# Gelu and sigmoid of a mixing phase by hyperbolic tangents, tile by tile, with the sums of the gated output asked for earlier

## The chip, the core and the metric

The program runs on one core of a Trainium2 chip. [...] An engine waits for another on semaphores. The metric is the device time of one execution in microseconds. Before the change three runs took 2308.72 to 2311.48 us, median 2311.45.

## The reference

One layer of a streaming encoder on 2048 tokens of 1024 features, float32. An input projection feeds two halves of 512 features: a state-space layer and chunked attention. The part that the change touches is what lies between them and the output projection:

```python
y = jax.nn.gelu(y.reshape(bsz, seq, D_SSM))                      # tanh form
y = y * jax.nn.sigmoid(y @ w_glu.astype(f32) + b_glu.astype(f32))
...
mixed = jnp.concatenate([rmsnorm(y_ssm, norm_ssm_out_g[l]),
                         rmsnorm(y_att, norm_att_out_g[l])], axis=-1)
x = x + mixed @ w_out[l]
```

After it come a SwiGLU layer, a residual and a last norm, which the change leaves as they are.

## The kernel before

Features lie on the 128 partitions, tokens along the free dimension. The mixing (mix_phase, from line 973) works on four blocks of 512 tokens, each with four tiles of 128 features (f or q from 0 to 3). Products that need float32 are made of a high and a low part (hi/lo, gh/gl, woh/wol): split makes the high part on ACT and the low part, raw minus high, on DVE or POOL; mm3 issues three matrix products (high by high, low weight or input by high).

For a block, load reads y, the state-space output, into yr, applies Gelu into ys and splits it into gh and gl. yr has its tokens in the order (j, c) and ys in the order (c, j), so Gelu's instruction reads yr in steps. load_a reads ya, the attention output, and squares makes its sum of squares over the four tiles: Squares on ACT, additions on DVE and, for tile 2, on POOL. glu multiplies by w_glu (4 tiles, each 4 quarters of 3 products, into ps), applies the sigmoid gate to ys, and calls squares on it. rstd1 sums the squares over the partitions (products with ones, into PSUM) and runs newton on DVE: 14 small steps, from nv to no, that give 1/rms. spread brings no to all partitions by PE, and rstd2 multiplies ys or ya by it and by the gain. mixed splits the outcome into m, and w_out multiplies m by the output weights, adds xt and stores x.

Tiles of one name share buffers in turn: sg has SGB = 2. sg holds the raw gate weights, the terms of squares and, in blocks 2 and 3, the gate.

Blocks 0 and 1 begin while attention still runs. There glu is called with late: the four tiles of ps get their bias on DVE and are put into yr; after the fourth, one instruction of ACT takes the sigmoid of all four, and DVE multiplies. load makes one instruction of Gelu over four tiles. In blocks 2 and 3 both go tile by tile. Gelu, Sigmoid and attention's Exp belong to different function tables of ACT; where the function changes, an ACT_TABLE_LOAD stands in its order.

What sets the order: PE's instructions keep the order in which the code is written. attention's loop runs in steps, and mix_phase is a generator whose yields are spread over the last steps, so that glu's quarters lie among scores (sc), transposes of the exponentials (pt), products with v (pj). In a step DVE makes scores plus bias and their minimum (s, mn), ACT the Exp, PE pt, ACT and DVE the high and low parts pth and ptl; for a pair of heads yt (ACT) and ya (DVE) follow. The other engines' instructions are placed by a scheduler when the program is built, and then run in that order. The sub-steps of block 1's glu are counted: at number R1 the sums of block 0's gated output are asked for (line 1171). Behind block 1's glu, w_out of block 0 starts with the attention half of m; the state-space half needs the spread.

## Time and profile before

| what | value |
|---|---|
| median of three runs | 2311.45 us |
| the profiled execution | 2304.9 us |
| its span, first to last instruction | 2303.1 us |
| mean clock of PE | 0.975 |
| ACT_TABLE_LOAD on ACT | 9, of 1.283 us each |
| the mixing, about | 686 to 950 us |

In the profile, a row of a timeline has start and length in us, engine, line, operation, tile written and tiles read, partitions by elements and a count; in brackets the idle time of the engine just ahead of it and what released it. A row of a group has the total, the mean in ns of one instruction, and the idle time ahead of them. A row of a table by stretches has each engine's busy time and, as PEclk, the share of full clock that PE was granted.

### The profile page before, as it was taken

Reading aid. Unit: us, or ns where it says so; the run is one execution under the profiler, and the core shown is the slowest. Engines: PE = TensorE matmul, PEld = TensorE weight load, DVE = VectorE, ACT = ScalarE, POOL = GpSimd, SP = SyncE. Lnnn points to the kernel's source line nnn. Section 1 sums busy time; section 2 is a strip of 40 time slices with the busy share of each in tenths; the row PEclk is TensorE's granted clock in tenths of the full one; section 3 lists DMA queues with packets and bytes.
Section 4 is the critical chain, followed back from the end, with each engine's and each line's share of the span. In section 5 each row is a group of like instructions: output and inputs, shape, how many; then the busy total and the mean of one; then the engine's idle time right before and its main releaser. Section 6 shows DMA issues by size and latency. Waiting matters only on the chain.

```text
span 2303.1 us, 30454 instructions
## 1 busy us (share of the span) xinstructions
PE 2183.8 (95%) x10568; PEld 1834.1 (80%) x10568; DVE 1487.8 (65%) x2286; ACT 1001.3 (43%) x1675; POOL 1061.0 (46%) x1245
## 2 busy tenths in 40 slices
PE   8978799999997899989999999999999999999997
PEld 6667688898986788778888887888888878888886
DVE  7845555656555756676775669766645376578676
ACT  6335555555557542343333335333333343344332
POOL 3416655455660433265555554555555314445442
PEclk9989999999998999999999999999999999999998
DMA  8788766766653534754554556555433287465552
GB/s 295 260 286 265 235 210 204 207 190 193 192 137 114 178 118 163 249 165 143 167 193 157 205 190 254 195 193 167 158 96 110 76 326 265 165 228 183 201 182 74
DMA packets 216370, 437.00 MB, mean 190 GB/s; under 512 B 27352, under 2 KB 58120, under 8 KB 209112
## 3 DMA queue, kind: packets, MB, share of 16 engines
q1 hardware_dynamic: 211352, 420.89, 55.0%
q0 software_dynamic: 4864, 14.17, 1.9%
q8 instruction: 83, 1.36, 0.2%
q14 instruction: 71, 0.58, 0.1%
HBM read 294.98 MB, written 132.15 MB: 185 GB/s over the span
## 4 chain that ended last, share of the span: by engine, by line
PE 59%; DVE 3%; DMA 1%; ACT 1%; issue 1%; POOL 1%; SPq 0%; DVEq 0%; ACTq 0%; POOLq 0%
PE X L74 20%; PE ps L74 18%; PE Y L74 10%; PE big L74 6%; PE W L74 5%; DVE acc L1575 1%; DMA lo<-hc 0%; DMA x<-xt 0%; DVE xt L1117 0%; DVE lo L166 0%; DVE hd L166 0%; POOL c L166 0%; ACT hi L165 0%; POOL sa L1125 0%; DMA gl<-x 0%
## 5 line engine op out<-in xcount | busy, mean ns | idle before, releaser
L74 PE MATMUL X<-hi,c 128*128 128x512 f32 x1408 | 452.2, 392 | 7.6 <-ACT u L1391 3.5
L74 PE MATMUL ps<-hd,hd 128*128 128x512 f32 (+1 forms) x1968 | 431.7, 381 | 3.9 <-DVE hd L166 3.7
L74 PEld LDWEIGHTS ps<-hd,hd 128*128 128x128 f32 x1968 | 358.8, 190 | 75.5 <-DVE hd L166 5.1
L166 POOL TENSOR_TENSOR c<-S,c 128x512 fp32r<-128x512 f32 x176 | 253.1, 1440 | 260.7 <-ACT c L165 258.8
L74 PEld LDWEIGHTS X<-hi,c 128*128 128x128 f32 x1408 | 265.8, 189 | 65.2 <-ACT u L1391 5.1
L74 PE MATMUL X<-lo,c 128*128 128x512 f32 x704 | 275.3, 391 | 0.0
L166 POOL TENSOR_TENSOR hd<-hd 128x1536 fp32r<-128x1536 f32 (+1 forms) x46 | 159.1, 3463 | 232.0 <-ACT hd L165 218.8
L166 POOL TENSOR_TENSOR c<-raw,c 128x512 fp32r<-128x512 f32 x132 | 189.0, 1432 | 137.5 <-ACT c L165 109.1
L165 ACT CAST hd<-hd 128x1536 fp32r<-128x1536 f32 (+1 forms) x106 | 147.4, 1393 | 219.4 <-DMA hd<-hq 134.5
L74 PE MATMUL Y<-hi,c 128*128 128x512 f32 x704 | 225.5, 391 | 4.8 <-DVE u L1395 4.8
L1521 DVE TENSOR_TENSOR acc<-acc,ps 128x512 f32<-128x512 f32 x196 | 129.2, 681 | 79.5 <-PE ps L74 79.1
L74 PE MATMUL big<-m,woh 128*128 128x512 f32 x512 | 165.4, 404 | 0.6 <-DVE m L166 0.4
L165 ACT CAST c<-S 128x512 fp32r<-128x512 f32 x176 | 109.5, 622 | 116.5 <-PE Y L74 59.1
L74 PE MATMUL pf<-hi,w 128*128 128x512 f32 x416 | 150.9, 415 | 9.4 <-ACT hi L729 5.8
L74 PEld LDWEIGHTS Y<-hi,c 128*128 128x128 f32 x704 | 132.6, 188 | 33.9 <-DVE u L1395 6.3
L74 PEld LDWEIGHTS X<-lo,c 128*128 128x128 f32 x704 | 133.0, 189 | 27.7
L1391 ACT COPY u<-X 128x512 f32<-128x512 f32 x132 | 77.1, 585 | 177.5 <-PE X L74 177.5
L846 DVE CUSTOM_DVE_ANT_0 s<-sc,nb 128x640 f32<-128x640 f32 (+4 forms) x128 | 94.4, 737 | 89.4 <-PE sc L74 85.9
L605 POOL TENSOR_TENSOR st<-X,a 128x128 f32<-128x128 f32 (+2 forms) x136 | 47.4, 349 | 220.0 <-ACT X L591 157.4
L165 ACT CAST c<-raw 128x512 fp32r<-128x512 f32 x132 | 82.1, 622 | 143.1 <-PE Y L74 80.3
L166 DVE TENSOR_TENSOR hd<-hd 128x1536 fp32r<-128x1536 f32 (+1 forms) x60 | 119.3, 1990 | 31.2 <-ACT hd L165 30.5
L74 PE MATMUL Y<-lo,c 128*128 128x512 f32 x352 | 137.2, 390 | 0.0
(462 smaller groups left out, 4644.2 us busy)
## 6 DMA issues: line engine op xcount, KB each, us to landing
w<-wss SPq DMA_DIRECT2D x36, 1024.0 KB, 5.5
hq<-g SPq DMA_DIRECT2D x140, 256.0 KB, 2.1
hd<-hq SPq DMA_DIRECT2D x42, 768.0 KB, 4.5
hd<-wc SPq DMA_DIRECT2D x42, 768.0 KB, 6.0
raw<-in_w_gate SPq DMA_DIRECT2D x44, 512.0 KB, 3.7
raw<-in_w_up SPq DMA_DIRECT2D x44, 512.0 KB, 4.1
wc<-px SPq DMA_DIRECT2D x66, 256.0 KB, 3.2
wss<-w SPq DMA_DIRECT2D x12, 1024.0 KB, 5.6
```

Of the source, the lines that this page charges most:

```text
L74: return self.tc.keep_in_program_order(self.tc.nc.tensor.matmul(*a, **b))
L165: (hi_eng or nc.scalar).copy(hi, raw)
L166: (lo_eng or nc.gpsimd).tensor_tensor(lo, raw, f32(hi), op=ALU.subtract)
L605: eng.tensor_tensor(t[:, :, :, :n], src, ar, op=ALU.mult)
L846: nc.vector.tensor_tensor_reduce(s[:, :nk].rearrange("p (a b) -> p a b", a=nch), ps[:, :nch, :half], hd.nb[:, nk - 1 :: -1].rearrange("p ( ...
L1391: nc.scalar.copy(u[:], ps[:])
L1521: V.tensor_tensor(a, a, ps[:], op=ALU.add)
L1575: nc.vector.scalar_tensor_tensor(v, v, k.go[:, i : i + 1], self.rs[:, : self.n], op0=ALU.mult, op1=ALU.mult)
```

## The change

Gelu's tanh form is written out: a Square of y on ACT, a product on DVE that also adds 1/0.044715, a Tanh on ACT, a product on DVE (tanh plus one, times y), which gives twice the Gelu. gh is then a scaled copy, and gl is made with a scale of 0.5 in its subtraction. The sigmoid is half of one plus tanh of half its argument: a Tanh on ACT that reads ps, with half the bias, and a product on DVE. So ys holds four times the gated output; a scale in squares and a quarter of the gain gs make up for it. Both go tile by tile in all blocks, the intermediate t and the gate in sg; yr no longer holds the gate. The instructions read yr in blocks of 64, and the second product writes ys in steps of eight elements. R1 goes from 13 to 9. The built program has two ACT_TABLE_LOADs, at the start and at Silu.

```diff
@@ -33,7 +33,8 @@
 LAG = 2
 WB = 3
 OPEN, GSTART = 119, 122
-R1 = 13
+R1 = 9
+CUBE = 0.044715
 SGB = 2
 ON_POOL = 2, 5, 7
 RA1, RA2 = 2, 12
@@ -982,6 +983,8 @@
         nc.sync.dma_start(gs[:], io["g_ssm"])
         nc.sync.dma_start(ga[:], io["g_att"])
         nc.sync.dma_start(bg[:], io["b_glu"])
+        nc.vector.tensor_scalar(gs[:], gs[:], 0.25, None, op0=ALU.mult)
+        nc.vector.tensor_scalar(bg[:], bg[:], 0.5, None, op0=ALU.mult)
         BIG = ("big", [P, 1024])
         W, Wg = {}, {}
 
@@ -1003,14 +1006,14 @@
                 raw = raws[n] if n < len(raws) else load_wo(n, wr, "xt")
                 split(k, W[q][0][:], W[q][1][:], raw[:], nc.vector if n % 2 else nc.gpsimd)
 
-        def squares(src):
+        def squares(src, scale=1.0):
             sq = k.t(mz, "sq", [P, SB], bufs=2)
             for f in range(4):
                 if f == 0:
-                    nc.scalar.activation(sq[:], src[f], AF.Square)
+                    nc.scalar.activation(sq[:], src[f], AF.Square, scale=scale)
                 else:
                     t = k.t(mz, "sg", [P, SB], bufs=SGB)
-                    nc.scalar.activation(t[:], src[f], AF.Square)
+                    nc.scalar.activation(t[:], src[f], AF.Square, scale=scale)
                     (nc.gpsimd if f == 2 else nc.vector).tensor_tensor(sq[:], sq[:], t[:], op=ALU.add)
             return sq
 
@@ -1019,7 +1022,7 @@
 
         yrs = [None]
 
-        def load(sb, one=False):
+        def load(sb):
             b = B()
             b.o = {}
             yt = k.t(my, "ys", [P, 4, SB], bufs=2)
@@ -1028,13 +1031,16 @@
                 yrs[0] = k.t(my, "yr", [P, 4, L, 128])
                 for f in range(4):
                     nc.sync.dma_start(yrs[0][:, f], S["y"][f * P : (f + 1) * P, :, sb * 64 : sb * 64 + 128])
-            yv = b.yr = yrs[0][:, :, :, (sb % 2) * 64 : (sb % 2 + 1) * 64]
-            fs = [slice(0, 4)] if one else [slice(f, f + 1) for f in range(4)]
-            for s in fs:
-                nc.scalar.activation(yt[:, s].rearrange("p f (c j) -> p f c j", j=L), yv[:, s].rearrange("p f j c -> p f c j"), AF.Gelu_apprx_tanh)
+            yv = yrs[0][:, :, :, (sb % 2) * 64 : (sb % 2 + 1) * 64]
             for f in range(4):
+                t = k.t(mz, "sg", [P, L, SB // L], bufs=SGB)
+                nc.scalar.activation(t[:], yv[:, f], AF.Square)
+                nc.vector.scalar_tensor_tensor(t[:], t[:], 1 / CUBE, yv[:, f], op0=ALU.add, op1=ALU.mult)
+                nc.scalar.activation(t[:], t[:], AF.Tanh, scale=CUBE * math.sqrt(2 / math.pi))
+                nc.vector.scalar_tensor_tensor(b.ys[f].rearrange("p (c j) -> p j c", j=L), t[:], 1.0, yv[:, f], op0=ALU.add, op1=ALU.mult)
                 gh, gl = k.t(my, f"gh{f}", [P, SB], F32R), k.t(my, f"gl{f}", [P, SB], F32R)
-                split(k, gh[:], gl[:], b.ys[f], nc.vector)
+                nc.scalar.activation(gh[:], b.ys[f], AF.Copy, scale=0.5)
+                nc.vector.scalar_tensor_tensor(gl[:], b.ys[f], 0.5, f32(gh[:]), op0=ALU.mult, op1=ALU.subtract)
                 b.g.append((gh, gl))
             return b
 
@@ -1044,11 +1050,7 @@
                 nc.sync.dma_start(b.ya[f], S["ya"][sb, f * P : (f + 1) * P])
             b.sqa = squares(b.ya)
 
-        def glu(b, bank, late=False):
-
-
-            def by8(a):
-                return a.rearrange("p (a b) -> p a b", a=L)
+        def glu(b, bank):
 
             for f in range(4):
                 ps = bank()
@@ -1057,18 +1059,11 @@
                     mm3(te, ps[:, :512], Wg[q][0][:, cs], Wg[q][1][:, cs], b.g[q][0][:], b.g[q][1][:], q == 0, q == 3)
                     if q < 3:
                         yield
-                if late:
-                    nc.vector.tensor_scalar(b.yr[:, f], by8(ps[:, :512]), bg[:, f : f + 1], None, op0=ALU.add)
-                    if f == 3:
-                        nc.scalar.activation(b.yr, b.yr, AF.Sigmoid)
-                        for i in range(4):
-                            nc.vector.tensor_tensor(by8(b.ys[i]), by8(b.ys[i]), b.yr[:, i], op=ALU.mult)
-                else:
-                    sg = k.t(mz, "sg", [P, SB], bufs=SGB)
-                    nc.scalar.activation(sg[:], ps[:, :512], AF.Sigmoid, bias=bg[:, f : f + 1])
-                    nc.vector.tensor_tensor(b.ys[f], b.ys[f], sg[:], op=ALU.mult)
+                sg = k.t(mz, "sg", [P, SB], bufs=SGB)
+                nc.scalar.activation(sg[:], ps[:, :512], AF.Tanh, bias=bg[:, f : f + 1], scale=0.5)
+                nc.vector.scalar_tensor_tensor(b.ys[f], sg[:], 1.0, b.ys[f], op0=ALU.add, op1=ALU.mult)
                 yield
-            b.sqs = squares(b.ys)
+            b.sqs = squares(b.ys, 0.25)
 
         def rstd1(b, c, ps):
 
@@ -1145,12 +1140,12 @@
         yield
         mw = rx.enter_context(tc.tile_pool(name="mw", reuse_waits="tile", bufs=2, side="right"))
         wr = rx.enter_context(tc.tile_pool(name="wr", reuse_waits="tile", bufs=2, side="right"))
-        b = load(0, True)
+        b = load(0)
         load_a(b, 0)
         raws = [load_wo(n, wr, "xt") for n in range(2)]
         for _ in range(PY):
             yield
-        for n, _ in enumerate(glu(b, bank, True)):
+        for n, _ in enumerate(glu(b, bank)):
             if n == RA1:
                 rstd1(b, 0, bank())
             if n == RA2:
@@ -1158,7 +1153,7 @@
                 spread(k, te, pb, b.o[0], 0)
                 rstd2(b, 0, pb[:])
             yield
-        nxt = load(1, True)
+        nxt = load(1)
         for _ in range(PZ):
             yield
 
@@ -1167,7 +1162,7 @@
             psum = k.psum
             return bank() if psum is None else big()
 
-        for n, _ in enumerate(glu(nxt, bk, True)):
+        for n, _ in enumerate(glu(nxt, bk)):
             if n == R1:
                 rstd1(b, 1, bk())
             yield
```

What the scheduler made of it, at three places. First DVE among the last steps of attention, behind the splits of the gate weights (wgl); ISA is the instruction that makes s and its minimum mn; the numbers in the names are those of buffers and differ between the two programs. Before:

```order
L166 TENSOR_TENSOR wgl_1899_8231<-sg_8232,wgh_1898_8230 128x512
L166 TENSOR_TENSOR wgl_1902_8237<-sg_8238,wgh_1901_8236 128x512
L889 TENSOR_TENSOR ya_8144<-pj_8314,yt_8331 64x512
L846 ISA s_8401,mn_8402<-sc_8396,nb_8133 128x640
L846 ISA mn_8402 128x1
L865 TENSOR_TENSOR ptl_8335<-pt_8336,pth_8334 128x5x128
L898 TENSOR_TENSOR ya_8144<-ya_8144,pj_8405 128x512
L846 ISA s_8425,mn_8426<-sc_8420,nb_8299 128x640
L846 ISA mn_8426 128x1
L865 TENSOR_TENSOR ptl_8335<-pt_8412,pth_8334 128x5x128
L865 TENSOR_TENSOR ptl_8335<-pt_8429,pth_8334 128x5x128
```

and now:

```order
L167 TENSOR_TENSOR wgl_1902_8239<-sg_8240,wgh_1901_8238 128x512
L1038 SCALAR_TENSOR_TENSOR sg_8358<-sg_8358,yr_8353 128x512
L1038 SCALAR_TENSOR_TENSOR sg_8367<-sg_8367,yr_8353 128x512
L890 TENSOR_TENSOR ya_8144<-pj_8316,yt_8333 64x512
L1040 SCALAR_TENSOR_TENSOR ys_8352<-sg_8358,yr_8353 128x8x64
L866 TENSOR_TENSOR ptl_8337<-pt_8338,pth_8336 128x5x128
L1040 SCALAR_TENSOR_TENSOR ys_8352<-sg_8367,yr_8353 128x8x64
L1043 SCALAR_TENSOR_TENSOR gl_1931_8364<-ys_8352,gh_1930_8363 128x512
L1038 SCALAR_TENSOR_TENSOR sg_8376<-sg_8376,yr_8353 128x512
L1043 SCALAR_TENSOR_TENSOR gl_1934_8373<-ys_8352,gh_1933_8372 128x512
L847 ISA s_8422,mn_8423<-sc_8417,nb_8133 128x640
L847 ISA mn_8423 128x1
```

Seven instructions of block 0's Gelu (lines 1038, 1040, 1043) have come ahead of the next minimum, in front of which only ya stood.

Second, ACT: Gelu and the high parts of block 1. Before, directly behind block 0's, ahead of the first Exp that follows (the sq and sg rows are Squares of the attention output):

```order
L165 CAST gh_1935_8369<-ys_8350 128x512
L1013 ACTIVATE sg_8383<-ya_1938_8374 128x512
L1013 ACTIVATE sg_8386<-ya_1939_8375 128x512
L1034 ACTIVATE ys_8631<-yr_8351 128x2048
L1013 ACTIVATE sg_8389<-ya_1940_8376 128x512
L849 ACT_TABLE_LOAD
L849 ACTIVATE s_8449,sm_8249<-s_8449,mn_8450 128x640
```

and now, behind the last gate tile of block 0 (sg from pf, line 1063) and the Squares of its gated output (line 1016):

```order
L1063 ACTIVATE sg_8641<-pf_8611,bg_8214 128x512
L1016 ACTIVATE sg_8646<-ys_8352 128x512
L1016 ACTIVATE sg_8649<-ys_8352 128x512
L1016 ACTIVATE sg_8652<-ys_8352 128x512
L1037 ACTIVATE sg_8656<-yr_8353 128x512
L1037 ACTIVATE sg_8665<-yr_8353 128x512
L889 COPY yt_8713<-pj_8696 64x512
L1039 ACTIVATE sg_8656<-sg_8656 128x512
L1039 ACTIVATE sg_8665<-sg_8665 128x512
L1042 ACTIVATE gh_1999_8661<-ys_8655 128x512
L1037 ACTIVATE sg_8674<-yr_8353 128x512
L1042 ACTIVATE gh_2002_8670<-ys_8655 128x512
```

Block 1's Gelu has moved from ahead of block 0's gate to behind it.

Third, DVE: the newton steps for block 0's gated output, among splits of the output weights (wol) and block 1's gate. Before:

```order
L1061 TENSOR_SCALAR yr_8351<-big_8709,bg_8214 128x8x64
L166 TENSOR_TENSOR wol_2031_8823<-m_2017_8792,woh_2030_8822 128x1024
L1061 TENSOR_SCALAR yr_8351<-big_8723,bg_8214 128x8x64
L115 TENSOR_SCALAR nv_8749<-big_8744 128x4
L166 TENSOR_TENSOR wol_2035_8831<-m_2019_8796,woh_2034_8830 128x1024
L116 CAST nf_8750<-nv_8749 128x4
L1061 TENSOR_SCALAR yr_8351<-big_8737,bg_8214 128x8x64
L117 TENSOR_SCALAR nf_8750<-nf_8750 128x4
L119 TENSOR_SCALAR nv_8749<-nv_8749 128x4
L118 CAST ny_8751<-nf_8750 128x4
```

and now:

```order
L1064 SCALAR_TENSOR_TENSOR ys_8655<-sg_8751,ys_8655 128x512
L167 TENSOR_TENSOR wol_2043_8861<-xt_8415,woh_2042_8860 128x1024
L1064 SCALAR_TENSOR_TENSOR ys_8655<-sg_8767,ys_8655 128x512
L116 TENSOR_SCALAR nv_8782<-big_8777 128x4
L117 CAST nf_8783<-nv_8782 128x4
L118 TENSOR_SCALAR nf_8783<-nf_8783 128x4
L120 TENSOR_SCALAR nv_8782<-nv_8782 128x4
L119 CAST ny_8784<-nf_8783 128x4
L122 TENSOR_TENSOR nf_8783<-ny_8784 128x4
L123 TENSOR_TENSOR nf_8783<-nf_8783,nv_8782 128x4
L124 SCALAR_TENSOR_TENSOR no_8785<-nf_8783,ny_8784 128x4
```

The additions of the bias (line 1061) are gone, products by the gate (line 1064) have come, and nv stands ahead of the second wol of these rows instead of the third. On PE the sums (four products of ones with sq) now stand behind the second quarter of block 1's tile 2, not the second of tile 3; PE's order is otherwise as it was. On SP the loads of y for block 2 stand ahead of those of xt.

## Prediction

> **What bounds the kernel now.** I read the page's busy times and its chain that ended last, then a table by stretches around the mixing, then the timelines of each engine there.
>
> ```profile
> PE 2183.8 (95%) x10568; PEld 1834.1 (80%) x10568; DVE 1487.8 (65%) x2286; ACT 1001.3 (43%) x1675; POOL 1061.0 (46%) x1245
> PE 59%; DVE 3%; DMA 1%; ACT 1%; issue 1%; POOL 1%; SPq 0%; DVEq 0%; ACTq 0%; POOLq 0%
> core 0: us, PE busy (x) PEld busy (x) DVE busy (x) ACT busy (x) POOL busy (x), PEclk, DMA share, GB/s
> 698.00:721.30 23.30, 10.89 (x44) 8.46 (x42) 10.41 (x18) 18.83 (x22) 1.28 (x1) 0.63 0.54 183
> ...
> 743.30:762.00 18.70, 18.01 (x83) 14.13 (x81) 17.92 (x18) 12.52 (x17) 14.45 (x7) 1.00 0.61 220
> 762.00:767.40 5.40, 0.29 (x3) 0.05 (x1) 5.09 (x16) 2.18 (x2) 2.50 (x1) 0.95 0.27 85
> 767.40:790.00 22.60, 21.34 (x95) 17.32 (x96) 17.24 (x23) 17.58 (x27) 7.79 (x5) 0.94 0.50 158
> 790.00:900.00 110.00, 109.75 (x504) 91.19 (x503) 62.96 (x141) 41.24 (x59) 36.77 (x26) 0.98 0.41 134
> ```
>
> TensorE is the bound and the chain is mostly its own work. The change can gain only where PE stands still in the mixing: 12.4 us of 698 to 721 and 5.1 us of 762 to 767. From 790 to 900 PE is never idle. Elsewhere the change can only cost. PE's waits in full:
>
> ```profile
> 701.72 1.00 PE L77 MATMUL pt<-ident,s 128*128 128x128 f32 x5 [2.42 <-DVE ptl L865]
> ...
> 705.54 1.30 PE L77 MATMUL pt<-ident,s 128*128 128x128 f32 x5 [1.75 <-DVE ptl L865]
> 713.61 0.79 PE L74 MATMUL pf<-gh,wgh 128*128 128x512 f32 x1 [6.76 <-ACT gh L165]
> ...
> 715.35 0.63 PE L74 MATMUL pf<-gh,wgh 128*128 128x512 f32 x1
> 715.78 0.63 PE L74 MATMUL pf<-gl,wgh 128*128 128x512 f32 x1
> ...
> 721.26 1.05 PE L74 MATMUL pf<-ones,sq 128*128 128x1 f32 x8 [1.47 <-DVE sq L1014]
> ...
> 739.29 0.40 PE L74 MATMUL pf<-gh,wgl 128*128 128x512 f32 x1
> ...
> 743.35 0.48 PE L74 MATMUL big<-gh,wgh 128*128 128x512 f32 x1
> ...
> 755.86 0.40 PE L74 MATMUL big<-gh,wgl 128*128 128x512 f32 x1
> ...
> 767.38 1.09 PE L77 MATMUL big<-ident,no 128*128 128x128 f32 x4 [5.11 <-DVE no L123]
> ...
> 788.39 1.05 PE L74 MATMUL big<-ones,sq 128*128 128x1 f32 x8 [1.16 <-DVE nv L115]
> ```
>
> A matmul of 512 columns follows the last after 0.43 us at the low clock (715.35, 715.78); 48 of them and the sums take 12.9 us at full clock (743.35 to 756.2), about 0.23 us each.
>
> ```profile
> L849 ACT ACTIVATE s<-s,mn 128x640 f32<-128x640 f32 x96 | 79.9, 833 | 51.8 <-DVE mn L846 51.5
> L864 ACT CAST pth<-pt 128x640 fp32r<-128x640 f32 x96 | 66.6, 693 | 59.9 <-PE pt L77 58.5
> ...
> 707.59 1.28 ACT L1034 ACT_TABLE_LOAD   x1
> 708.88 3.64 ACT L1034 ACTIVATE ys<-yr 128x2048 f32<-128x2048 f32 x1
> ...
> 712.95 2.16 ACT L165 CAST gh<-ys 128x512 fp32r<-128x512 f32 x4
> 716.07 3.83 ACT L1034 ACTIVATE ys<-yr 128x2048 f32<-128x2048 f32 x1
> ...
> 776.40 1.28 ACT L1034 ACT_TABLE_LOAD   x1 [1.11 <-issue]
> ...
> 826.30 1.28 ACT L1068 ACT_TABLE_LOAD   x1
> ...
> 700.00 0.82 DVE L846 CUSTOM_DVE_ANT_0 s<-sc,nb 128x640 f32<-128x640 f32 x1
> ```
>
> The 6.8 us wait is a table load (1.28), one Gelu over four tiles (3.64), and gh. Yet block 1's Gelu (716.07) also runs here, 27 us before PE needs it at 743.35: that cover the change gives up. Four of the seven table loads that go, those of blocks 2 and 3 (776.40 to 826.30), fall where PE hardly waits: they are worth nothing.
>
> **Prices.** The new instructions by their nearest rows:
>
> ```profile
> L1013 ACT ACTIVATE sg<-ys 128x512 f32<-128x512 f32 x12 | 7.4, 632 | 5.3 <-DVE ys L1069 4.7 <-DVE sq L1014 0.6
> L1082 DVE SCALAR_TENSOR_TENSOR ys<-ys,gs,big 128x512 f32<-128x512 f32 x16 | 10.8, 737 | 0.0
> 746.85 1.29 POOL L1014 TENSOR_TENSOR sq<-sq,sg 128x512 f32<-128x512 f32 x1 [28.65 <-DVE sq L1014]
> L1117 DVE TENSOR_TENSOR xt<-xt,big 128x1024 f32<-128x1024 f32 x16 | 19.4, 1214 | 38.6 <-PE big L74 29.3 <-DMA xt<-in_xt 9.2
> L88 ACT COPY rsn<-pb 128x512 f32<-128x512 f32 x4 | 4.9, 1222 | 0.1
> L88 ACT COPY pb<-pp 128x512 f32<-128x512 f32 x4 | 2.3, 587 | 26.6 <-PE pp L77 26.6
> ```
>
> A Square, tanh or scaled copy on ACT is 0.63 us (0.52 apart in a row: 2.16 for four gh). A plain product on DVE is 0.74 (0.66 apart: 10.8 us for 16), an addition on POOL 1.29. The two scalings of gs and bg are four columns wide (nv below, as wide, takes 0.14): nothing. Per block DVE gets eight more instructions (products), of which four write ys with a step of eight elements. The trace has no such write on DVE; the nearest is ACT's copy to rsn, which steps by eight (1.22 us against 0.59 for a plain one). So such a product lies between 0.74 (as if plain) and 1.48 (twice); I take 1.22.
>
> [...]
>
> **Term A, block 0, up to the sums of the attention output (PE row 721.26): +2.3.** (sc are scores, pt their transposes, ptl the low part, exp the softmax's exponential.) The added DVE rows stand between wgl and the softmax's next minimum: five plain (0.66) and two stepped (1.22), 5.7 us. The minimum moves from 700.0 to 706.1, and the third pt behind it (ptl, exp, one more stepped product) from 705.5 to 709.4. PE then finds gh and gl of tiles 0 and 1 ready, so the 6.8 us wait goes: six matmuls at 0.43, scores and pt (about 1.05 each at this clock, as at 701.72), until 715.3. But ACT's order puts the Squares of the attention output behind the third exp; pth (0.69) and that exp (0.83) follow on this pt, until 716.9. From there: Square 0.6, product 0.7, tanh 0.65, stepped product 1.25, gh 0.6, Square 0.6, POOL 1.3, DVE 0.75, handoffs: 723.6 against 721.3. The first wait is replaced by one of about 7 us on the sums. From there to the last gate matmul (739.7) PE works without a break; DVE trades four bias additions for four products. So that end, T0, is 742.0.
>
> **Term B, block 1: +9.9.** Its Gelu uses the two sg buffers, behind the gate and the squares of block 0, so it can't start before T0. The chain: tanh 742.7, product 743.5, Square of the third tile 744.2, POOL's addition 745.6 (frees sg), Square 746.3, product 747.05, tanh behind yt 748.1, ya 748.35, stepped product 749.6, gh 750.2. PE's cover, the last attention products, ran from 739.7 to 743.35: until 745.65 now. Then DVE has, in order, a stepped product (to 750.75), ya (751.3), two gl (752.55), two products (753.8), two stepped (756.3), m (756.95), two gl (758.2). PE ends the first gate tile at 759.1, in pieces, at the low clock. Six more matmuls at 0.43 and 30 at 0.23 end at 768.4; before it was 756.2. That is 12.2 late, of which 2.3 is term A.
>
> **Term C, the sums of the gated output: −6.1.**
>
> ```profile
> 759.54 0.14 DVE L115 TENSOR_SCALAR nv<-big 128x4 f32<-128x4 f32 x1
> 759.61 2.70 DVE L166 TENSOR_TENSOR wol<-m,woh 128x1024 fp32r<-128x1024 f32 x1
> 762.23 2.30 DVE L116 CAST nf<-nv 128x4 f32<-128x4 int32 x1
> 764.44 0.74 DVE L1061 TENSOR_SCALAR yr<-big,bg 128x512 f32<-128x512 f32 x1
> ...
> 767.07 0.16 DVE L123 SCALAR_TENSOR_TENSOR no<-nf,ny 128x4 f32<-128x4 f32 x1
> ```
>
> Newton's 14 steps were asked for late and stood among two weight splits and a bias addition, so PE waited 5.1 us at 767.38. Now the sums come after gate tile 2's second quarter (about 765), the steps end near 770, and PE wants them at 768.4 plus the first half of the first output product (24 matmuls, 5.6): 774.0. The wait goes, with 1.0 of the 1.4 us that clock 0.94 over 22.6 us cost behind it. Next late is then m of the gated output, which PE wants 5.5 us later, as before; it costs what it did.
>
> **Term E, the pair of sums at 788.39: +1.3.** PE writes the second sums only when DVE's nv has read the first. From the spread at 774.0 PE needs 0.7, 24 and 48 matmuls (16.6 with the stalls on m that the row pattern has today, 1.2), and 0.9 for the first sums: 793.4. DVE makes the four gains until 780.3 (they stand behind POOL's addition of block 1's squares), two m and an addition until 782.9, then block 2's products: four plain 2.65, four stepped 4.9, two gl 1.3; then two additions to x (1.2 each) and two gl (1.3) stand before nv: 795.6. A wait of about 2.5 in place of 1.16. Blocks 2 and 3 have 20 to 30 us of cover for gh (PE never idle from 790 to 900): nothing. Without that cover block 3 would pay block 1's price. SP's queue: yr is free once ys is made, so block 2's loads of y go ahead of those of xt; both are wanted 25 us later: nothing.
>
> **Sum.** +2.3 +9.9 −6.1 +1.3 = +7.4 us. The profiled execution took 2304.9 (span 2303.1 and 1.8 around it): 2312.3. The median of the runs, 2311.45, lies 6.55 above that execution, so I forecast 2318.9. With stepped products at 1.48 the eleven in the way (3, 4, 4) add 2.9: 2321.8.
>
> **Rivals.**
> - Stepped writes cost 0.74. A is −0.5 (sums at 720.8), B +8.1 (gate ends 763.8 from T0 739.2), C −6.1, E 0: +1.5, 2313.0. For it: no row on DVE speaks against it. Against: the copy to rsn, and Gelu itself, which reads in steps (3.64 for 2048 elements).
> - Faster: the first wait really goes. DVE was free for 12.9 of the 23.3 us from 698 to 721. If the products fall into those holes, PE gets from 706.8 to the sums by 714.7, A is −6.6, and with PE busy there the clock of 0.63 recovers for 1.5 more: −8.1 +8.1 −6.1 +0 = −6.1, 2305.4. It decides whether the attention output's sums are ready before 715. Against it: those Squares stand behind the third exp.
> - Newton is still last, between two products that wait for tanh: C is 0, +13.5, 2325. Against it: PE has 8 us of work behind tile 2.
>
> That the table loads stay is excluded: the built order has two where there were nine.
>
> **How the numbers follow.** Forecast 0.48 (2315 to 2323), plain writes 0.25 (2309 to 2316), faster 0.20 (2302 to 2309), Newton 0.07. From 2307 to 2323 only 0.15 of the third case and 0.05 at the top are left out. This kernel's measurement tells 0.2% (4.6 us) from no change: below 2306.8 lies 0.15 (third case); above 2316.1 lie 0.41 of the forecast and 0.07 of the last, 0.48; within, 0.37.
>
> **What would show it.** A: PE waits some 7 us for sq ahead of the first sums, none for gh before. B: waits for gh and gl at block 1's first gate tile, with a lower clock up to 760. C: no wait before the first spread of block 0's gated sums. E: the wait on nv near 790 at 2 to 3 us. Stepped products: their group's mean near 1.2. The forecast is wrong if the attention sums come before 715, or if block 1's gh is there when PE ends the attention products.

## The result, and the profile after

The changed kernel took 2322.69 us (median of 8 runs, 2318.77 to 2327.34) against 2312.16 (8 runs, 2305.87 to 2317.13) for the kernel before: a ratio of 1.0043, 95% interval 1.0028 to 1.0057. It is slower, as forecast, and inside the range, 0.3 us below its upper end of 2323; it lies 3.8 us above the forecast of 2318.9.

The profiled execution took 2320.35 us, span 2318.6, where the one before had a span of 2303.1. This is the page's busy line after:

```profile
PE 2192.6 (95%) x10568; PEld 1841.2 (79%) x10568; DVE 1513.1 (65%) x2312; ACT 997.5 (43%) x1696; POOL 1053.1 (45%) x1245
```

In all rows PE is the engine of the matrix products (results in PSUM), PEld its weight loads, DVE VectorE, ACT ScalarE, POOL GpSimd, and SP the engine that issues transfers.

DVE has 25.3 us more work, ACT 3.8 less. The table by stretches, over the stretches that the prediction showed of before, says where PE stood:

```profile
core 0: us, PE busy (x) PEld busy (x) DVE busy (x) ACT busy (x) POOL busy (x), PEclk, DMA share, GB/s
698.00:721.30 23.30, 14.40 (x71) 11.97 (x69) 16.54 (x27) 16.06 (x31) 0.00 (x0) 0.75 0.59 179
743.30:762.00 18.70, 11.38 (x39) 7.82 (x38) 16.32 (x22) 13.84 (x24) 4.16 (x3) 0.70 0.35 126
762.00:767.40 5.40, 5.40 (x23) 4.34 (x22) 4.48 (x3) 3.41 (x6) 3.32 (x2) 0.78 0.20 37
767.40:790.00 22.60, 20.39 (x85) 15.76 (x84) 20.22 (x29) 13.11 (x20) 13.39 (x7) 0.92 0.72 224
790.00:900.00 110.00, 107.22 (x488) 89.28 (x488) 75.01 (x143) 44.76 (x72) 37.29 (x26) 0.97 0.32 104
```

Block 1's gate stretch, 743 to 762, was full before (PE 18.01 of 18.70 at clock 1.00). Now PE works 11.38 of it at clock 0.70. The hole at 762 to 767 is gone, but 767 to 790 has not become full: 2.2 us of it are still idle. From 790 to 900, where PE was idle for 0.25 us, 2.8 us are idle now. PE's timeline after, with the start of each stage and each of its waits in the mixing from the first sums on:

```profile
694.89 1.06 PE L75 MATMUL pj<-U,Tm 128*128 128x256 f32 x2
...
712.80 0.77 PE L75 MATMUL pf<-gh,wgh 128*128 128x512 f32 x1
...
725.18 1.86 PE L75 MATMUL pf<-ones,sq 128*128 128x1 f32 x8 [7.18 <-DVE sq L1017]
...
744.03 0.39 PE L75 MATMUL pf<-gh,wgl 128*128 128x512 f32 x1
...
752.63 0.80 PE L75 MATMUL big<-gh,wgh 128*128 128x512 f32 x1 [4.29 <-ACT gh L1042]
754.01 0.79 PE L75 MATMUL big<-gl,wgh 128*128 128x512 f32 x1 [0.59 <-DVE gl L1043]
757.67 0.79 PE L75 MATMUL big<-gh,wgh 128*128 128x512 f32 x1 [1.15 <-ACT gh L1042]
759.05 0.80 PE L75 MATMUL big<-gl,wgh 128*128 128x512 f32 x1 [0.59 <-DVE gl L1043]
...
771.73 0.39 PE L75 MATMUL big<-gh,wgl 128*128 128x512 f32 x1
...
776.64 0.50 PE L75 MATMUL big<-m,wol 128*128 128x512 f32 x1 [2.03 <-DVE wol L167]
...
781.18 0.74 PE L78 MATMUL big<-ident,no 128*128 128x128 f32 x4
...
802.44 1.87 PE L75 MATMUL big<-ones,sq 128*128 128x1 f32 x8 [2.48 <-DVE nv L116]
...
962.79 1.05 PE L75 MATMUL big<-ones,sa 128*128 128x1 f32 x8 [2.33 <-POOL sa L1120]
```

I measure stages between such rows: U (694.89, the last sequence product's first row, at the head of the mixing), T0 (744.03), the end of block 1's gate (771.73 and 0.23 more), the spread (781.18), the second of the pair of sums (802.44), and the last sums of sa (962.79), the end of the mixing. Before, the rows stood at 691.00, 739.29, 755.86 (so 756.09), 767.38, 788.39 and 947.32. What follows the last row takes 1355.8 us in both. U itself is 3.9 later after; over all kernels of this study it lies anywhere from 690.3 to 697.7 without regard to the change, so I leave it out. The stages give 256.3 before and 267.9 after: **11.6 us**, close to the 10.5 between the medians. In the table, differences are taken before rounding, and the forecast of C is split as the prediction splits it: 5.1 for the wait ahead of the spread, 1.0 for the clock behind the spread.

| stage, us | before | after | difference | forecast |
|---|---|---|---|---|
| U to T0 (term A) | 48.3 | 49.1 | +0.8 | +2.3 |
| T0 to the end of block 1's gate (B) | 16.8 | 27.9 | +11.1 | +9.9 |
| gate's end to the spread (C) | 11.3 | 9.2 | −2.1 | −5.1 |
| spread to the second sums (C's clock and E) | 21.0 | 21.3 | +0.3 | −1.0 and +1.3 |
| second sums to the end (E) | 158.9 | 160.4 | +1.4 | 0 |

A and B are near. E's wait is 2.48 us, forecast 2.5. Step C is the one that went wrong: the wait on Newton is gone, but of the 5.1 us that this was to gain ahead of the spread 3.0 are not there.

### The profile page after: what moved, and what is told of

Same layout as the page of the kernel before. It is cut to its first block, busy times and chain, and to the rows that moved or that the text cites. A ratio compares the mean times of both kernels' runs of the same rounds, so it can differ in the third digit from the quotient of the medians.

```text
span 2318.6 us, 30509 instructions
## 1 busy us (share of the span) xinstructions
PE 2192.6 (95%) x10568; PEld 1841.2 (79%) x10568; DVE 1513.1 (65%) x2312; ACT 997.5 (43%) x1696; POOL 1053.1 (45%) x1245
## 4 chain that ended last, share of the span: by engine, by line
PE 51%; DVE 2%; DMA 1%; POOL 1%; ACT 0%; issue 0%; SPq 0%; DVEq 0%; ACTq 0%
PE X L75 19%; PE ps L75 17%; PE Y L75 10%; PE W L75 5%; DMA lo<-hc 1%; DVE lo L167 1%; DVE acc L1570 1%; DMA hd<-wc 0%; POOL c L167 0%; DMA acc<-x 0%; DVE hd L167 0%; DVE u L1390 0%; SPq L1332 0%; ACT hi L166 0%; DVE g L1433 0%
## 5 line engine op out<-in xcount | busy, mean ns | idle before, releaser
L75 PE MATMUL X<-hi,c 128*128 128x512 f32 x1408 | 452.3, 392 | 10.4 <-ACT c L166 4.9
```

Of the source, the lines that this page charges most:

```text
L75: return self.tc.keep_in_program_order(self.tc.nc.tensor.matmul(*a, **b))
```

## The experiments

All kernels were timed in five rounds beside the kernel before, whose median in the three sets was 2310.3, 2310.5 and 2310.4 (2309.3 for the last kernel). Compare by ratios: the intervals are about ±0.12%, 3 us. The stages of one profile carry about as much. The first four expectations name five theories. O: block 1's Gelu stands behind block 0's gate through the sg buffers, and early sums gain little, as Newton and the weight splits stand in each other's way. S: the early sums are worth the whole wait of 5 us. N: they are worth nothing. G: the tile-wise gate is itself the cost. V: the added DVE products cost wherever they stand.

| kernel | median, us | ratio and interval | U to T0 | to gate's end | to spread | to second sums | to end | U to end |
|---|---|---|---|---|---|---|---|---|
| r1_alone | 2310.93 | 1.0000 [0.9989, 1.0011] | 48.1 | 16.8 | 11.8 | 22.4 | 160.6 | 259.7 |
| gate_alone | 2309.99 | 0.9999 [0.9987, 1.0011] | 48.3 | 16.5 | 11.8 | 20.6 | 160.2 | 257.3 |
| gelu_alone | 2326.44 | 1.0068 [1.0048, 1.0088] | 48.9 | 35.0 | 5.5 | 22.9 | 161.3 | 273.6 |
| own_buffer | 2316.94 | 1.0026 [1.0015, 1.0038] | 49.2 | 16.8 | 13.5 | 23.8 | 161.5 | 264.7 |
| newton_psum | 2330.96 | 1.0091 [1.0077, 1.0104] | 50.9 | 26.9 | 7.0 | 26.6 | 168.4 | 279.9 |
| own_psum | 2324.02 | 1.0069 [1.0056, 1.0082] | 49.5 | 17.2 | 11.7 | 27.4 | 168.5 | 274.2 |
| r13_back | 2323.00 | 1.0053 [1.0039, 1.0067] | 50.0 | 27.0 | 11.4 | 20.2 | 160.6 | 269.1 |
| plain_write | 2316.12 | 1.0030 [1.0018, 1.0042] | 48.4 | 25.7 | 9.7 | 19.9 | 158.7 | 262.4 |
| after_dve | 2313.97 | 1.0021 [1.0006, 1.0035] | 50.5 | 28.0 | 7.8 | 18.8 | 157.6 | 262.7 |
| gate_dve | 2307.85 | 0.9980 [0.9966, 0.9994] | 48.2 | 16.5 | 9.0 | 19.7 | 157.3 | 250.7 |
| before_dve | 2313.03 | 1.0013 [1.0003, 1.0022] | 48.3 | 16.8 | 13.3 | 20.4 | 160.7 | 259.4 |
| own_dve | 2312.92 | 1.0010 [0.9998, 1.0021] | 49.0 | 17.1 | 10.4 | 21.9 | 160.5 | 258.8 |

**The parts one at a time.** *r1_alone* is the kernel before with the earlier sums and nothing else.

```diff
-R1 = 13
+R1 = 9
```

> The kernel before with R1 = 9 alone. Theory O (order: what the change lost, it lost because block 1's Gelu moved behind block 0's gate; the earlier sums gain little, since newton and the weight splits stand in each other's way on DVE): 0 to 3 us faster than before, with a new wait of PE on a weight split in place of the 5.1 us on newton. Rival S (the earlier sums are worth their whole wait): 5 us faster. Rival N (nothing: DVE is full there, and what is done earlier delays the rest as much): within 1 us.

PE still waited for Newton ahead of the spread, 5.58 us against 5.11, and the time did not move. Theory S is refuted: the sums were asked for sooner, and Newton was not done sooner. The time is what N had; O's range allows it, but the wait on a weight split that O named did not come.

*gate_alone* keeps the Gelu of before, and has the tanh gate tile by tile with the early sums.

```diff
...
-                    sg = k.t(mz, "sg", [P, SB], bufs=SGB)
-                    nc.scalar.activation(sg[:], ps[:, :512], AF.Sigmoid, bias=bg[:, f : f + 1])
-                    nc.vector.tensor_tensor(b.ys[f], b.ys[f], sg[:], op=ALU.mult)
+                sg = k.t(mz, "sg", [P, SB], bufs=SGB)
+                nc.scalar.activation(sg[:], ps[:, :512], AF.Tanh, bias=bg[:, f : f + 1], scale=0.5)
+                nc.vector.scalar_tensor_tensor(b.ys[f], sg[:], 1.0, b.ys[f], op0=ALU.add, op1=ALU.mult)
```

> The gate by Tanh, tile by tile, and R1 = 9, with Gelu left as it was before (one table function, four tiles at once in blocks 0 and 1). Theory O: block 1's Gelu keeps its early place, so term B (11 us) is absent, and bias additions leave DVE: 2 to 6 us faster than before, 2306 to 2310. Rival G (the tile-by-tile gate is itself what costs, as its Tanh waits for each tile between other work of ACT): 3 us or more slower than before.

The gate costs nothing and gains nothing, so G falls; the 2 to 6 us that O had it gain did not come either. The wait on Newton has gone, and another has taken its place, of 3.99 us for VectorE's first weight split.

*gelu_alone* is the other half: the Gelu written out, with the late gate in one Sigmoid over four tiles and the sums where they were (R1 at 13). Its edit on the kernel before is the change's loop in `load`, with these lines at its core:

```diff
-                nc.scalar.activation(yt[:, s].rearrange("p f (c j) -> p f c j", j=L), yv[:, s].rearrange("p f j c -> p f c j"), AF.Gelu_apprx_tanh)
...
+                t = k.t(mz, "sg", [P, L, SB // L], bufs=SGB)
...
+                nc.scalar.activation(t[:], t[:], AF.Tanh, scale=CUBE * math.sqrt(2 / math.pi))
```

> Gelu written out, with the gate of before (Sigmoid, late, R1 = 13). Theory O: block 1's Gelu stands behind the squares of block 0, which now come only after the one late Sigmoid: 10 to 16 us slower than before, 2322 to 2328, PE waiting for gh at the first gate tile of block 1. Rival V (the added products on DVE cost what they last, wherever they stand, about 6 us in the way): 2316 to 2320.

The whole loss and more. PE's timeline has the first and the last of four waits in block 1's gate:

```profile
754.37 0.79 PE L75 MATMUL big<-gh,wgh 128*128 128x512 f32 x1 [8.40 <-ACT gh L1041]
...
765.49 0.79 PE L75 MATMUL big<-gl,wgh 128*128 128x512 f32 x1 [2.79 <-DVE gl L1042]
```

*own_buffer* is the changed kernel with one edit: the Gelu's intermediate no longer takes sg.

```diff
-                t = k.t(mz, "sg", [P, L, SB // L], bufs=SGB)
+                t = k.t(mz, "tg", [P, L, SB // L], bufs=1)
```

> The changed kernel, with one buffer of its own for Gelu's intermediate t in place of the two of sg. The built order then has block 1's Gelu among block 0's gate again; the work is the same. Theory O: 8 to 11 us less than the changed kernel, 2311 to 2315, PE not waiting for gh at block 1's first gate tile. Rival V (the DVE work itself): 2320 to 2324, as changed.

Block 1's gate is back at 16.8 us, with the same instructions and only another buffer. So term B is the sg buffers, as the prediction had it, and V falls. But of these 11 us the whole time shows little, 3.9 by the ratios (5.8 between the medians, taken in different sets), and the two intervals overlap. The two waits that PE meets afterwards are longer than the changed kernel's 2.03 and 2.48: now 5.22 (for wol, in the rows below of PE's timeline in own_buffer) and 4.77 (for nv).

```profile
759.24 0.39 PE L75 MATMUL big<-gh,wgl 128*128 128x512 f32 x1
...
765.99 0.80 PE L75 MATMUL big<-m,wol 128*128 128x512 f32 x1 [5.22 <-DVE wol L167]
```

**Why Newton and the weight splits are late.** In the changed kernel's DVE timeline, Newton's steps behind the early sums read so:

```profile
767.91 0.16 DVE L116 TENSOR_SCALAR nv<-big 128x4 f32<-128x4 f32 x1 [0.69 <-PE big L75]
768.10 1.83 DVE L117 CAST nf<-nv 128x4 f32<-128x4 int32 x1
769.96 2.32 DVE L118 TENSOR_SCALAR nf<-nf 128x4 f32<-128x4 f32 x1
772.20 0.15 DVE L120 TENSOR_SCALAR nv<-nv 128x4 f32<-128x4 f32 x1
772.32 2.33 DVE L119 CAST ny<-nf 128x4 int32<-128x4 f32 x1
...
775.36 1.23 DVE L167 TENSOR_TENSOR wol<-m,woh 128x1024 fp32r<-128x1024 f32 x1
```

Three steps of four columns take about 2 us each, the others 0.16. The last row is the weight split that PE waits for at 776.64; it stands behind these steps. POOL's timeline over the same time:

```profile
767.50 2.41 POOL L167 TENSOR_TENSOR wol<-m,woh 128x1024 fp32r<-128x1024 f32 x1 [2.18 <-ACT woh L166]
769.86 2.40 POOL L167 TENSOR_TENSOR wol<-m,woh 128x1024 fp32r<-128x1024 f32 x1
772.23 2.41 POOL L167 TENSOR_TENSOR wol<-xt,woh 128x1024 fp32r<-128x1024 f32 x1
```

The ends are the thing to read. POOL's weight splits end at 769.91, 772.26 and 774.64; the slow steps at 769.93, 772.28 and 774.65. Each step ends 0.01 to 0.02 us behind a split of POOL. *newton_psum* puts the first operands of Newton into the PSUM tile of the sums, so that the casts are no longer from SBUF to SBUF.

```diff
+    x, pv, pf = ps[:, :w], ps[:, 16 : 16 + w], ps[:, 32 : 32 + w]
...
-    V.tensor_copy(f[:], v[:].bitcast(I32))
-    V.tensor_scalar(f[:], f[:], -0.5, 1597463007.0, op0=ALU.mult, op1=ALU.add)
-    V.tensor_copy(y[:].bitcast(I32), f[:])
-    V.tensor_scalar(v[:], v[:], -0.5, None, op0=ALU.mult)
+    V.tensor_copy(pf, pv.bitcast(I32))
+    V.tensor_scalar(pf, pf, -0.5, 1597463007.0, op0=ALU.mult, op1=ALU.add)
+    V.tensor_copy(y[:].bitcast(I32), pf)
+    V.tensor_scalar(v[:], x, -0.5 / n, -0.5 * EPS, op0=ALU.mult, op1=ALU.add)
```

> The changed kernel; Newton's start (value, cast, scaling, cast back) keeps its four columns in the PSUM tile of the sums, not in SBUF. In the changed kernel three of these steps took 1.83, 2.32 and 2.33 us, each ending where one of POOL's weight splits ended. Theory H (a one-source step from SBUF to SBUF on VectorE is held until POOL's running instruction ends): each takes under 0.3 us now, Newton ends 5 to 6 us earlier than 777.9, the weight splits behind it come earlier, PE's wait of 2.03 on wol goes or shrinks below 0.7, and the time is 2319.5 to 2321.5. Rival W (the steps are slow for some other reason, or the weight splits take up what Newton gives up): steps stay at 1.8 us or more, or they shrink and the wait on wol stays; 2322 to 2324.

Its DVE timeline:

```profile
764.87 0.17 DVE L135 TENSOR_SCALAR big<-big 128x4 f32<-128x4 f32 x1
765.07 0.16 DVE L136 CAST ny<-big 128x4 int32<-128x4 f32 x1
...
765.27 1.57 DVE L139 TENSOR_TENSOR nf<-ny 128x4 f32<-128x4 f32 x1
766.88 2.32 DVE L140 TENSOR_TENSOR nf<-nf,nv 128x4 f32<-128x4 f32 x1
769.12 1.21 DVE L184 TENSOR_TENSOR wol<-m,woh 128x1024 fp32r<-128x1024 f32 x1
770.26 2.37 DVE L141 SCALAR_TENSOR_TENSOR no<-nf,ny 128x4 f32<-128x4 f32 x1
```

and its POOL timeline:

```profile
764.04 2.78 POOL L184 TENSOR_TENSOR wol<-m,woh 128x1024 fp32r<-128x1024 f32 x1 [1.17 <-ACT woh L183]
766.78 2.40 POOL L184 TENSOR_TENSOR wol<-m,woh 128x1024 fp32r<-128x1024 f32 x1
769.14 3.47 POOL L184 TENSOR_TENSOR wol<-xt,woh 128x1024 fp32r<-128x1024 f32 x1
```

Half of theory H holds: with an operand in PSUM the casts take 0.16 to 0.17 in the midst of a split of POOL. The other half was too narrow: the next three steps, with two inputs in SBUF, are now held instead, and end at 766.84, 769.20 and 772.63 where POOL's splits end at 766.82, 769.18 and 772.61. The hold has moved by four instructions, not gone. The time of 2331 is no verdict on it, for the edit has a cost of its own that I had not priced: it stands in every block, the last step that reads the sums is now the fifth (L137) and not the first, and PE waits for it at all three pairs of sums (5.94, 2.47 and 2.48 us, where the changed kernel has one wait over 0.5, of 2.48).

*own_psum* is the same edit on own_buffer.

> The version with a buffer of its own for the Gelu's intermediate, with Newton's start in PSUM as well. There PE waited 5.22 us for the first weight split of VectorE, which stood behind three Newton steps of 2.19, 2.30 and 2.26 us. Theory H: the steps take under 0.3 us, that split comes about 4 us earlier (it will itself take some 2.8 beside POOL where it took 1.22 alone), the wait falls to 0.5 to 2, and the time from 2316.9 to 2312.5 to 2315. Rival W: the wait stays above 4, and the time within 1.5 of 2316.9.

The same: casts of 0.17, then three steps of 1.57, 2.30 and 2.26, the wait on wol 4.42 and that on nv 7.28. Theory H's forecast (2312.5 to 2315) missed for the same reason.

*r13_back* is the changed kernel with the sums back at 13.

```diff
-R1 = 9
+R1 = 13
```

> The changed kernel with the sums of the gated output asked for where they were before (13 for 9). The prediction's step C put their move at 6.1 us: by it 2327.5 to 2330. By the two traces the move was worth about 2 us, since Newton then stood beside POOL's weight splits and put the weight splits off: 2323.5 to 2326, with PE waiting 3 to 6 us for Newton ahead of the first spread. If the move is worth nothing: 2321.5 to 2323.5.

PE's timeline there:

```profile
783.56 1.09 PE L78 MATMUL big<-ident,no 128*128 128x128 f32 x4 [5.73 <-DVE no L124]
...
803.79 1.14 PE L75 MATMUL big<-ones,sq 128*128 128x1 f32 x8 [0.60 <-DVE nv L116]
```

The wait on Newton is back, yet the ratio (1.0053) is that of the changed kernel within the intervals. Of what the early sums gain at the spread (2.2 us) 1.0 goes before the next meeting is over, where nv is behind block 2's products and PE, being sooner, waits 2.48 instead of 0.60; the rest is less than the runs can tell. So the move of the sums was worth nothing that can be measured in the changed kernel either.

*plain_write* asks what the step of eight costs; it leaves out the reordering of the tokens.

```diff
-                nc.vector.scalar_tensor_tensor(b.ys[f].rearrange("p (c j) -> p j c", j=L), t[:], 1.0, yv[:, f], op0=ALU.add, op1=ALU.mult)
+                nc.vector.scalar_tensor_tensor(b.ys[f].rearrange("p (j c) -> p j c", j=L), t[:], 1.0, yv[:, f], op0=ALU.add, op1=ALU.mult)
```

> The changed kernel with the Gelu's last product written in the order in which it is read (no step of eight); the tokens of ys then stand in another order, so the output is not the reference's. Those products took 1.08 us in the changed kernel where the plain ones took 0.68. If the stepped write is what costs 0.4: 0.68 now, and with about ten of them in PE's way, partly covered, 2318.5 to 2321. If the 0.4 lies in the stepped reading of y instead (which stays): still 1.08, and 2322 to 2323.5. The copy to gh and the low part read ys in line in both.

The group's row in the changed kernel (total, mean in ns):

```profile
L1040 DVE SCALAR_TENSOR_TENSOR ys<-sg,yr 128x512 f32<-128x512 f32 x16 | 17.0, 1126 | 0.9 <-ACT sg L1039 0.7
```

and in plain_write:

```profile
L1040 DVE SCALAR_TENSOR_TENSOR ys<-sg,yr 128x512 f32<-128x512 f32 x16 | 10.9, 689 | 1.2 <-ACT sg L1039 0.7
```

The stepped write is 0.44 us of each product, and the reading of y has no part in it. The stages sum to 5.5 us less than the changed kernel's, 2.2 of it in B; the ratio falls from 1.0043 to 1.0030, and the two intervals overlap. The median, 2316.1, is below what I expected.

**Without POOL's splits.** The last four kernels give all eight weight splits to VectorE, so that POOL hardly works beside Newton.

```diff
-                split(k, W[q][0][:], W[q][1][:], raw[:], nc.vector if n % 2 else nc.gpsimd)
+                split(k, W[q][0][:], W[q][1][:], raw[:], nc.vector)
```

*after_dve* is that on the changed kernel.

> The changed kernel with all eight weight splits of the output product on VectorE (before: every second one on POOL). Theory X: a VectorE instruction whose operands all lie in SBUF and a product on POOL never run at once, each waits for the other's end. Then the splits take 1.22 each in place of 2.4 on POOL and 2.7 beside POOL, the thirteen small Newton steps behind nv take under 0.2 each (1.83, 2.32, 2.33 for three of them in the changed kernel), the wait of 2.03 on wol is under 0.5, and PE reaches the first spread 2 to 4 us earlier against T0. Part of it comes back as a longer wait on nv at the pair of sums (2.48 now): 2319 to 2322. Rival Y (four more splits are simply more work for the busier VectorE): the wait on wol grows, 2323 to 2327.

Newton's first steps in its DVE timeline, with the splits that now stand between them:

```profile
767.05 0.16 DVE L116 TENSOR_SCALAR nv<-big 128x4 f32<-128x4 f32 x1 [1.61 <-PE big L75]
...
767.72 0.16 DVE L117 CAST nf<-nv 128x4 f32<-128x4 int32 x1
767.79 1.22 DVE L167 TENSOR_TENSOR wol<-m,woh 128x1024 fp32r<-128x1024 f32 x1
768.93 0.16 DVE L118 TENSOR_SCALAR nf<-nf 128x4 f32<-128x4 f32 x1
...
769.07 1.22 DVE L167 TENSOR_TENSOR wol<-m,woh 128x1024 fp32r<-128x1024 f32 x1
770.21 0.16 DVE L119 CAST ny<-nf 128x4 int32<-128x4 f32 x1
```

Every step is 0.16 and every split 1.22, but for a split at 760.27 (2.29) and a step at 774.65 (1.26), which ran beside POOL's m and POOL's addition. The wait on wol is gone. The gain, 5 us by the ratios and 5.2 by the stages (8.7 between the medians, taken in different sets), is more than the 1 to 4 expected: the wait on nv has shrunk to 0.96 and did not grow. One thing is not as expected: PE waits 2.22 for Newton at the spread, since the splits stand between Newton's steps.

*gate_dve* is the edit on gate_alone.

> The version with the Gelu of before and the tanh gate tile by tile with early sums, and all eight weight splits on VectorE. There PE waited 3.99 us for the first split, behind three held Newton steps (2.20, 2.34, 2.39). Theory X: no held steps, wait on wol under 1.5, 2306.5 to 2309.5, the fastest of all so far. Rival Y: the wait is 3.5 or more, 2310 to 2313.

As expected in time: 2307.85, ratio 0.9980 with an interval below one, the only version that beats both kernels. The wait for the first split is gone; there is one of 3.43 on Newton in its place, for the reason just given.

*before_dve* is the edit on the kernel before.

> The kernel before with all eight weight splits on VectorE and nothing else. Theory X: its Newton cast (2.30, held by POOL) takes under 0.2, its splits 1.22 in place of 2.70 to 2.76, and the wait of 5.11 for Newton falls to 1 to 3: 2307 to 2309.5. Rival Y: the wait on Newton is 5 or more, 2310 to 2313.

The durations came as theory X has them (the cast 0.15, the splits 1.17 to 1.22), the time did not: 1.0013, slower. With late sums the splits stand ahead of Newton and between its steps, and PE waits 7.64 for it instead of 5.11. In these kernels freeing DVE of the hold was worth something only together with sums that come early; gate_dve has the tanh gate besides, so that the early sums are the reason is argued, not shown.

*own_dve* is the changed kernel with both: the Gelu's own buffer, and the splits on VectorE.

> The changed kernel with both found costs taken out at once: a buffer of its own for the Gelu's intermediate (that alone 2316.9), and all eight weight splits on VectorE (that alone 2314.0; the changed kernel 2322.7). If both act at their own places: T0 to the end of block 1's gate 16.8 us (27.9 in the changed kernel), from there to the spread 8 to 10.5 (13.5 with the buffer alone), and 2310.5 to 2313.5; what is left over the kernel before would be the stepped products and the wait on nv at the pair of sums, near 5 us. If they act on the same time (PE, sooner at the pair of sums, only waits longer there for nv): a wait there of 7 or more and 2314.5 to 2317.

PE's timeline there:

```profile
746.64 0.40 PE L75 MATMUL pf<-gh,wgl 128*128 128x512 f32 x1
...
763.49 0.39 PE L75 MATMUL big<-gh,wgl 128*128 128x512 f32 x1
...
767.15 0.50 PE L75 MATMUL big<-m,wol 128*128 128x512 f32 x1 [0.79 <-DVE wol L167]
...
774.08 1.08 PE L78 MATMUL big<-ident,no 128*128 128x128 f32 x4 [3.65 <-DVE no L124]
```

The two costs act at their own places, as the first case of the expectation has it: block 1's gate takes 17.1 us, the stretch behind it 10.4, and the wait on nv at the pair of sums is 1.65. The time is 2312.92, and the interval of the ratio holds one: with these two causes out, the loss can't be told from nothing. 2.5 us of the stages' 11.6 remain.

## Why the prediction was right, and where it was not

**Bound, and where the change can act.** Right. Apart from the 3.9 us by which U itself is later, all of the difference lies between U and the end of the mixing; behind it the two kernels take the same 1355.8 us.

**Term A, forecast +2.3, measured +0.8.** The waits are as written: no wait ahead of the first gate product (712.80), and 7.18 us on the sums of the attention output (forecast about 7). So the table loads buy nothing here, as forecast. But the 2.3 are not where I had them. From U to these sums it took 30.3 us in both kernels: the softmax's next minimum (708.60) came 13.7 us behind U, where I had 15.1, and the exp ahead of the Squares ended 23.9 behind it, where I had 25.9. The 0.8 came behind the sums, where I had nothing: 18.8 us to T0 at a granted clock of 0.86, against 18.0 at 0.91. That is a cost and not the spread of single profiles: in all nine kernels with the Gelu written out this stretch takes 18.7 us or more, in the other five 18.2 or less. That it comes from the lower clock, and the clock from the longer wait, is argued from these figures.

**Term B, forecast +9.9, measured +11.1.** Right, and own_buffer shows the cause. The ACT timeline of the changed kernel has the chain that was forecast:

```profile
744.52 0.69 ACT L1063 ACTIVATE sg<-pf,bg 128x512 f32<-128x512 f32 x1 [0.75 <-PE pf L75]
...
748.00 1.36 ACT L1037 ACTIVATE sg<-yr 128x512 f32<-128x512 f32 x2 [0.80 <-POOL sq L1017]
...
749.87 1.15 ACT L1039 ACTIVATE sg<-sg 128x512 f32<-128x512 f32 x2
751.94 0.63 ACT L1042 ACTIVATE gh<-ys 128x512 fp32r<-128x512 f32 x1 [0.93 <-DVE ys L1040]
```

The Gelu's Square starts when POOL's addition frees sg, 3.6 us behind the end of T0's row (forecast 3.6), and the first gh starts 7.5 behind it (forecast 7.6). PE begins the gate 8.2 behind it (forecast 8.2). The 1.2 that the forecast fell short are in the last sum: behind 759.1, six products at 0.43 and 30 at 0.23 end at 768.6, not 768.4, and the row of the sums, which stands among them and takes 0.81 us, was left out.

**Term C, forecast −6.1, measured −3.2.** The part behind the spread came: to the first sums PE took 17.8 us at a granted clock of 0.99, against 18.9 at 0.92 before. The part ahead of the spread, the wait of 5.1, is the step that failed, and its mechanism failed with it: it gained 2.1. The prediction had "the steps end near 770", 5 us behind the sums. The sums came at 766.92 and Newton ended at 777.9, 11 us behind. I had read the cast of 2.30 us in before's rows (nf<-nv at 762.23) as a place in DVE's queue. It was held beside a split of POOL: it ended at 764.53, where that split ended at 764.50, and in before_dve it takes 0.15. Asking for the sums earlier put more of Newton's steps beside POOL's splits: one held step before, two in r1_alone, three in the changed kernel, in gate_alone and in own_buffer. And the held steps put off DVE's own splits, so that PE, no longer waiting for Newton, waited for wol instead, 2.03 us. The other 1.0 of the 3.0 that are missing is PE's own work: the thirteen products between that wait and the spread took 4.54 us at a granted clock of 0.66, 0.35 each. The prediction said that next late is m of the gated output; it was wol.

Of the steps beside POOL's splits, three with one input, from SBUF to SBUF, took 1.83 to 2.33 us in the changed kernel, those with a PSUM operand 0.15 to 0.17 in newton_psum, and the next three there, with inputs from SBUF alone, 1.57 to 2.37. Why a step is held no run here shows.

**Term E, forecast +1.3, measured +2.7.** The wait is right: 2.48 on nv, 1.3 more than before. The clock behind it was left out: from the second sums to the next such pair PE took 61.9 us at 0.95, against 60.6 at 0.97. r13_back shows what the wait is: not a cost of its own but the place where an earlier PE meets DVE. C and E together were forecast as −4.8 and measured as −0.4.

**Stepped products, taken at 1.22, bounds 0.74 and 1.48.** The mean was 1.126, and 0.689 when plain. The step of eight elements does cost, by a factor of 1.63, where ACT's copy to rsn, by which the prediction went, took 2.08 times as long as a plain one (1222 ns against 587). The rival with plain writes was priced at +1.5 and came out at +5.6 in plain_write's median against the kernel before; most of what it missed is term C, which it shared.

**The other rivals.** Newton did not end last (no wait at 781.18), so that price (+13.5) was not paid, though Newton was far later than forecast. By the time alone this rival (2325) is nearer to the measured 2322.7 than the forecast is; it is the rows that tell them apart. The first wait did not go, it changed its place. The 1.5 us that the faster rival's sum takes from the clock were an estimate; from 698 to 721 PE was busy for 14.40 us at 0.75, and before for 10.89 at 0.63.

**The sum and the range.** The sum of +7.4 was 4.2 short of the stages' 11.6: C missed by 3.0, E by 1.4 and B by 1.2 on one side, A by 1.5 on the other. That the time still lies inside the range is in part luck: the dearest case that the prediction works out below its upper end is that of stepped products at 1.48 (2321.8), and they came out cheaper than the forecast had them.

**Left open.** How much of after_dve's 5 us is the hold and how much the shorter splits (2.4 on POOL, 1.22 on VectorE): the edit takes away both, and newton_psum, meant to part them, moved the hold instead.

## What to carry to other kernels

When a wait ends last on a chain of small instructions, look first at their lengths: a four-column step of 2 us, 0.16 elsewhere in the same trace, is not computing, and here its end, 0.01 to 0.02 us behind a split of POOL, pointed to POOL; asking for its input sooner put two such steps beside POOL's splits instead of one (r1_alone). Before a scratch buffer is lent to a new step, list who held it last: two sg buffers cost 11 us of one stage here, since they tied work that was ready 27 us ahead to the end of another chain. And what is gained at one meeting of two engines has to be followed to the next, where the earlier engine may just wait again.

## What the runs showed of the hardware

In the mixing of these traces VectorE's splits, which read and write SBUF alone, and POOL's took longer beside each other. In the kernel before, VectorE's took 2.70 to 2.76 us there, and two of POOL's 6.34; with POOL idle VectorE's took 1.22 (after_dve), and beside nothing but four-column steps POOL's took 2.40 to 2.41 (the changed kernel, from 767.50). In a chain of small steps the difference is larger: four-column steps from SBUF to SBUF, 0.16 otherwise, took up to 2.39 beside a split of POOL (gate_alone, 755.93) and 1.26 beside an addition of 1.28 there (before, 790.83). The additions of the bias, which read PSUM, were not longer: 0.74 in the midst of POOL's splits (before, 755.53), 0.73 with POOL idle (before_dve, 756.15). That the two engines took turns, instruction by instruction, is argued from these lengths and from the ends. With four more splits on VectorE the changed kernel was 5 us faster by the ratios, though VectorE was the busier of the two.
